# Low parts of the up-projection's weights made by adding DMAs, 1/rms on VectorE, a third tile for the weight sums, and P4's low products last

## The chip, the cores and the metric

The kernel runs on one core of a Trainium2 chip. The metric is device time in microseconds (us) of one execution, shown as the median of the runs with the lowest and the highest.

The core's engines work in parallel, each through its own queue in order: PE (TensorE: matmuls from on-chip memory into accumulators), DVE (VectorE: elementwise), ACT (ScalarE: one-input elementwise), POOL (GpSimd: elementwise, and it can issue DMAs), SP (SyncE: here it only issues DMAs). Engines wait for one another through semaphores. 16 DMA engines move data.

## The reference

One layer of a hybrid decoder on 1024 tokens with 1024 channels, in float32:

```python
xn = rmsnorm(x, norm_mix_w); proj = xn @ w_in
merged = sigmoid(g_da) * (y_da @ w_br_da) + sigmoid(g_sw) * (y_sw @ w_br_sw)   # two attentions
x = x + merged @ w_mix_out
xn = rmsnorm(x, norm_ffn_w)
u = xn @ w_up                                   # 1024 -> 2 * 2816 channels
c = conv_b + sum(upad[:, j:j + S] * conv_w[j] for j in range(3))   # causal, per channel
gate, val = split(c, 2)
x = x + (silu(gate) * val) @ w_down
out = rmsnorm(x, norm_final_w)
```

The change lies in the stage that computes `u` and the convolution with its gate.

## The kernel before, in words

**Three passes.** A float32 operand is split into a high part `h` (rounded to the matmul's format by a copy on ScalarE, a CAST in the profile) and a low part `l` = value - `h` (a subtraction on VectorE). A product of two operands is `wh*xh + wh*xl + wl*xh`: three matmuls for every 128 rows of the inner dimension.

**Seven products for eight.** The up-projection's 5632 output channels are worked off as 22 pairs of blocks of 128 channels: pair j holds block j (gate, called g) and block j + 22 (value, called v). The inner dimension is cut in two halves of four chunks, and the tokens in two halves of 512 as well. Instead of eight products per pair there are seven, P1 to P7, each of 12 matmuls (four chunks by three passes) into one 128x512 accumulator. Their weight operands are A11, A12 (the two halves of g), A22 (the second half of v) and four sums S1 to S4, made by four operations of POOL of 128x512 each (`sum_pair`): `sa` holds S1 and S2, `sb` holds S3 and S4. `recombine` adds the seven results up into two tiles `us` of 128x1024 on VectorE.

In the order of the loop a pair's products are P1 (A11), P2 (A12), P5 (S1), P6 (S2), P7 (S3), P3 (S4), P4 (A22). In `product`, `low_last=True` puts the four matmuls with the weights' low part behind the eight others; before, only P1 has that.

**High and low parts of a pair's weights** are made in `split_pair`: four splits a pair, of g (128x1024, tiles wh and wl), `sa` and `sb` (128x1024 each, tiles sh and sl) and the second half of v (128x512, tiles wh and wl of the pool `w22`). Buffers set the order: wh and wl of g have two, sh and sl three between `sa` and `sb`, A22's wh and wl one; g is loaded into "raw" (three buffers), v into "rv" (two), and the sums lie in "sf" (two tiles, one for `sa`, one for `sb`). SP issues both loads and stores the finished rows of h to `hd` in DRAM. `ahead` keeps two pairs of weights in preparation: while pair j is multiplied, pair j + 1 and a part of j + 2 are prepared.

**After the products.** `glu_halves` multiplies both `us` tiles by 1/rms (`rstd`; 128x1024 on POOL, line 1083; for the first pair on VectorE), clears two border columns (a memset on POOL, line 1082), and runs the convolution: an activation on ScalarE (line 1089) and two scaled additions on VectorE (line 1091) per tile and half, then silu and the product of both.

The instructions are laid out by a tile framework, which sets the order within each engine from the order in the program, its priorities and the buffers, and writes the semaphore waits.

Of the kernel before, what the change touches and what calls it, by code (L numbers as in the profile page):

```python
# [10 lines left out]
F32 = mybir.dt.float32  # L11
F32R = mybir.dt.float32r
AF = mybir.ActivationFunctionType
ALU = mybir.AluOpType
# [3 lines left out]
P = 128  # L18
# [6 lines left out]
NF = DFF // P  # L25
# [19 lines left out]
class Trunk:  # L45
    def __init__(self, tc, ins, out):
        self.tc, self.nc = tc, tc.nc
        (self.xT, self.w_in, self.w_br, self.w_mix, self.w_up, self.w_dn,
         self.vecs_d, self.bias_d) = ins
        self.out = out  # L50
        self.uid = 0
        self.stores = []
        self.uw = self.w22 = self.behind = None
        self.pin, self.after = False, None
        self.hs, self.defer, self.late = {}, [], []

    def name(self, s):
# [12 lines left out]
    def ahead(self, n):  # L70
        while len(self.wq) < n and self.wsrc and (self.wsrc[0][1] != "pair" or self.uw):
            src, nk, *eng = self.wsrc.pop(0)
            if nk == "sums":

                self.sums = self.split_pair(*self.sum_pair(src, True, "sl"), 1, 3)
            elif nk == "rest":
                self.sums["A22"] = self.load_w(src[1][:, 4:8], 4)
                self.wq.append(self.sums)
            elif nk == "second":
                self.wq.append(self.second_pair(src, *eng))  # L80
            elif nk == "idle":
                self.wq.append(self.load_w(src, 8, None, (self.uw, "sh", "sl")))
            elif nk == "pair":
                first, skip = eng or (False, 0)
                self.wq.append(self.split_pair(*self.sum_pair(src, first), skip))
            else:
                self.wq.append(self.load_w(src, nk, *eng))
        if self.deep and self.wsrc and len(self.wsrc[0]) == 2 and not isinstance(self.wsrc[0][1], str):

            src, nk = self.wsrc[0]  # L90
            self.wsrc[0] = src, nk, None, None, self.load_raw(src, nk)

    def sum_pair(self, src, first=False, idle=None):


        nc = self.nc
        g = self.tl(self.wp, [P, 2, 4, P], "raw", bufs=RAW)
        nc.sync.dma_start(g.rearrange("p a k c -> p (a k) c"), src[0])
        v = self.tl(self.wp, [P, 2, 4, P], "raw", bufs=RAW) if first and not idle else self.tl(self.uw, [P, 2, 4, P], idle or "rv", bufs=2)
        nc.sync.dma_start(v.rearrange("p a k c -> p (a k) c"), src[1])  # L100
        sa, sb = (self.tl(self.sfp[0], [P, 2, 4, P], self.sfp[1]) for _ in range(2))
        tt = nc.gpsimd.tensor_tensor
        i = tt(sa[:, 0], v[:, 0], v[:, 1], ALU.add)  # L103
        if self.behind is not None:
            self.tc.add_manual_dep(i.ins, self.behind.ins.name, mybir.DependencyInfo(mybir.DependencyClass.Sync, mybir.DependencyReason.DATA), reason="operands first")
            self.behind = None
        tt(sa[:, 1], sa[:, 0], g[:, 0], ALU.subtract)
        tt(sb[:, 0], g[:, 0], v[:, 0], ALU.subtract)  # L108
        tt(sb[:, 1], g[:, 1], sa[:, 1], ALU.subtract)
        return g, v, sa, sb  # L110

    def split_pair(self, g, v, sa, sb, skip=0, end=4):

        nc = self.nc
        ops = {}
        for pool, h, l, src, names in ((self.wp, "wh", "wl", g, ("A11", "A12")), (self.uw, "sh", "sl", sa, ("S1", "S2")),
                                       (self.uw, "sh", "sl", sb, ("S3", "S4")), (self.w22 or self.wp, "wh", "wl", v[:, 1:2], ("A22",)))[skip:end]:
            n = len(names)
            hi = self.tl(pool, [P, n, 4, P], h, F32R)
            lo = self.tl(pool, [P, n, 4, P], l, F32R)  # L120
            with ExitStack() as queue:
                if self.pin and ops:
                    for i in done:
                        queue.enter_context(self.tc.issue_after(i.ins))
                if self.after is not None and names[0] == "A11":
                    queue.enter_context(self.tc.issue_after(self.after.ins))
                i = nc.scalar.copy(hi, src)  # L127
                j = nc.vector.tensor_tensor(lo, src, hi.bitcast(F32), ALU.subtract)  # L128
            if not ops:
                done = i, j  # L130
            if names[0] in ("A11", "A22"):
                ops["made", names[0]] = i, j
            for i, name in enumerate(names):
                ops[name] = hi[:, i], lo[:, i]
        self.pin, self.after = False, None
        return ops
# [788 lines left out]
    def hidden(self, pair):  # L925
        nc, tc = self.nc, self.tc
        with ExitStack() as ctx:
# [11 lines left out]
            for j in range(NF):  # L939
                w, ps = ready.pop(j) if j else (w0, {})  # L940
                if j == 0:
# [4 lines left out]
                    for k in range(4):  # L946
                        hi, lo = self.split(*(xc2.tile([P, T], F32R, name=f"T42_{k}{p}") for p in "hl"), self.t42[k])
# [14 lines left out]
                if j == NF - 1:  # L962

                    with tc.high_priority(50):
# [4 lines left out]
                        lo = self.lo  # L969
                for name, a, b in (prods[i] for i in ((0, 1, 2, 5, 3, 6, 4) if j == NF - 1 else (0, 1, 2, 5, 3, 4, 6) if j else range(7))):  # L970
                    if name not in ps:
                        ps[name] = self.tl(*((self.psC, [P, H2], "c") if j == 0 and name == "P4" else (psF, [P, H2], "t")))
                        self.product(ps[name], w[a], b, low_last=name == "P1")
                us = [self.tl(tp, [P, T + 2], "us", bufs=3) for _ in range(2)]
                if j == NF - 1:
                    self.defer.pop(0)(lo)
# [9 lines left out]
                if j < NF - 1:  # L986

                    self.after = c21
                    w, ps = ready[j + 1] = self.next_w(), {}
# [87 lines left out]
    def glu_halves(self, j, us):  # L1077

        nc = self.nc
        col = lambda m, k: self.vecs[:, C_CW + 3 * m + k:C_CW + 3 * m + k + 1]  # L1080
        for w, u in enumerate(us):
            nc.gpsimd.memset(u[:, 0:2], 0.0)
            (nc.vector if j == 0 else nc.gpsimd).tensor_tensor(u[:, 2:], u[:, 2:], self.rstd, ALU.mult)  # L1083
        out = self.tl(self.cpl, [P, T], "c")
        for o in (0, H2):
            cs = [self.tl(self.psC, [P, H2], "c") for _ in range(2)]
            for w, (u, c) in enumerate(zip(us, cs)):
                m = j + w * NF
                nc.scalar.activation(c, u[:, o + 2:o + 2 + H2], AF.Identity, bias=self.vecs[:, C_CB + m:C_CB + m + 1], scale=col(m, 2))  # L1089
                for k in (1, 0):  # L1090
                    nc.vector.scalar_tensor_tensor(c, u[:, o + k:o + k + H2], col(m, k), c, ALU.mult, ALU.add)  # L1091
            g = out[:, o:o + H2]
            nc.scalar.activation(g, cs[0], AF.Silu)  # L1093
            nc.vector.tensor_tensor(g, g, cs[1], ALU.mult)
        nc.sync.dma_start(self.hd[j], out)
# [351 lines left out]
```

## Time and profile before

| what | value |
|---|---|
| median of 3 runs (lowest to highest) | 1343.09 us (1341.19 to 1344.43) |
| profiled execution: its time / its span | 1342.84 us / 1340.6 us |
| up-projection on TensorE, from its first matmul to the down projection's | about 684 to 1106 us of the span |
| mean granted TensorE clock | 0.997 of full speed |

A row of the profile's groups reads: line, engine, operation, output<-input tiles, shapes, count | busy us in all, mean ns of one | idle time of the engine just before these instructions and what ended it. A row in order of time gives start and duration in us. In the waits, "A <- B" says that A was idle until B had finished. PEld is the load of weights, which runs beside the matmuls.

### The profile page before, as it was taken

The page shows a single profiled execution, that of the slowest core. Times are in us where ns is not written, and L with a number is a line of the kernel's source. Part 1 is how long each engine was busy: PE and PEld are TensorE (multiplying, and loading weights), DVE is VectorE, ACT ScalarE, POOL GpSimd, SP SyncE. Part 2 cuts the span into 40 slices and gives each one's busy share as a digit, 9 for nine tenths or more (in the row PEclk, how much of TensorE's full clock was granted, in tenths as well). Part 3 has the DMA queues.
Part 4 walks back from the last instruction along what each step waited for, and adds up shares of the span by engine and source line. Part 5 has one row for each costly group of instructions (what it writes and reads, how often), then busy time and mean ns, then how long its engine had stood idle before and what let it go on. Part 6 is the DMA issues. An engine that isn't in the chain of part 4 may idle for free.

```text
span 1340.6 us, 17301 instructions
## 1 busy us (share of the span) xinstructions
PE 1319.9 (98%) x6264; PEld 1097.0 (82%) x6264; DVE 1069.3 (80%) x1605; ACT 621.2 (46%) x1019; POOL 497.0 (37%) x365
## 2 busy tenths in 40 slices
PE   8999999999999999999999999999999999999997
PEld 6888888888888777878888888888888888888787
DVE  8847775289889876465678999999999997978985
ACT  9432232276667765333444443444443444323454
POOL 0336553001102124651446555655565510215422
PEclk9999999999999999999999999999999999999998
DMA  7423443876553235334432222222222229671333
GB/s 258 145 107 143 156 158 141 246 182 186 144 135 124 97 119 203 141 110 157 126 110 95 78 95 79 94 68 90 90 85 80 85 82 337 214 263 63 112 124 126
DMA packets 63045, 182.64 MB, mean 136 GB/s; under 512 B 6896, under 2 KB 15216, under 8 KB 62960
## 3 DMA queue, kind: packets, MB, share of 16 engines
q1 hardware_dynamic: 51504, 164.13, 37.5%
q10 hardware_dynamic: 11456, 17.41, 3.6%
q8 instruction: 49, 0.80, 0.3%
q14 instruction: 36, 0.29, 0.1%
HBM read 130.66 MB, written 50.86 MB: 135 GB/s over the span
## 4 chain that ended last, share of the span: by engine, by line
PE 87%; POOL 4%; DVE 4%; DMA 3%; ACT 1%; issue 1%; POOLq 0%; SPq 0%; ACTq 0%; DVEq 0%
PE t L920 13%; PE t L921 13%; PE t L922 13%; PE g L209 3%; PE t L914 3%; PE g L210 3%; PE g L211 3%; PE sc L636 3%; PE y L1159 2%; PE d L1159 2%; DMA gr<-gd 2%; PE sc L211 2%; PE sc L209 2%; PE sc L210 2%; PE d L920 2%; PE d L921 2%
## 5 line engine op out<-in xcount | busy, mean ns | idle before, releaser
L1089 ACT ACTIVATE c<-us,vecs 128x512 f32<-128x512 f32 x80 | 61.3, 780 | 133.2 <-POOL us L1083 129.2
L1091 DVE SCALAR_TENSOR_TENSOR c<-us,vecs,c 128x512 f32<-128x512 f32 x160 | 110.4, 747 | 8.6 <-ACT c L1089 8.5
L1083 POOL TENSOR_TENSOR us<-us,rstd 128x1024 f32<-128x1024 f32 x38 | 99.7, 2643 | 4.5 <-DVE us L469 2.4
L128 DVE TENSOR_TENSOR sl<-sf,sh 128x1024 fp32r<-128x1024 f32 x62 | 87.6, 1415 | 11.5 <-ACT sh L127 11.5
L127 ACT CAST sh<-sf 128x1024 fp32r<-128x1024 f32 x62 | 63.3, 1048 | 60.2 <-PE t L921 43.7
L176 DVE TENSOR_TENSOR wl<-raw,wh 128x1024 fp32r<-128x1024 f32 (+2 forms) x46 | 55.7, 1210 | 31.8 <-ACT wh L174 20.2
L128 DVE TENSOR_TENSOR wl<-raw,wh 128x1024 fp32r<-128x1024 f32 (+1 forms) x35 | 76.3, 2180 | 3.7 <-ACT wh L127 3.6
L103 POOL TENSOR_TENSOR sf<-rv 128x512 f32<-128x512 f32 x30 | 41.3, 1378 | 100.9 <-DVE sl L128 57.8
L174 ACT CAST wh<-raw 128x1024 fp32r<-128x1024 f32 (+2 forms) x46 | 46.1, 1001 | 61.8 <-PE sc L210 30.5
L209 PE MATMUL g<-xh,wh 128*128 128x512 f32 x176 | 70.6, 401 | 0.1
L211 PE MATMUL g<-xh,wl 128*128 128x512 f32 x176 | 70.3, 400 | 0.0
L210 PE MATMUL g<-xl,wh 128*128 128x512 f32 x176 | 70.3, 399 | 0.0
L108 POOL TENSOR_TENSOR sf<-raw,rv 128x512 f32<-128x512 f32 x30 | 40.7, 1358 | 65.3 <-DVE sl L128 65.3
L619 POOL MEMSET aT<- 128x128 f32 x32 | 6.2, 206 | 151.6 <-PE t L665 101.3
L640 DVE CUSTOM_DVE_ANT_0 L<-sc,bias 128x128 f32<-128x128 f32 (+7 forms) x64 | 47.7, 751 | 17.0 <-PE sc L636 13.7
L641 ACT ACTIVATE L<-L,sm 128x128 f32<-128x128 f32 (+7 forms) x64 | 49.6, 778 | 20.0 <-DVE sm L640 17.3
L794 POOL TENSOR_TENSOR gr<-gr,rstd 128x1024 f32<-128x1024 f32 x16 | 40.6, 2540 | 42.5 <-DMA gr<-gd 42.3
L1093 ACT ACTIVATE c<-c 128x512 f32<-128x512 f32 x40 | 24.0, 599 | 60.7 <-DVE c L1091 60.7
L128 DVE TENSOR_TENSOR wl<-rv,wh 128x512 fp32r<-128x512 f32 x30 | 49.3, 1642 | 3.5 <-ACT wh L127 3.5
L636 PE MATMUL sc<-u,u 128*128 128x512 f32 (+2 forms) x192 | 49.8, 358 | 0.0
L211 PE MATMUL sc<-mh,wl 128*128 128x512 f32 x126 | 49.1, 390 | 0.5 <-DVE wl L176 0.5
L209 PE MATMUL sc<-mh,wh 128*128 128x512 f32 x126 | 49.0, 389 | 0.0
(527 smaller groups left out, 4400.3 us busy)
## 6 DMA issues: line engine op xcount, KB each, us to landing
u<-qd SPq DMA_DIRECT2D x72, 256.0 KB, 6.6
raw<-in_w_in SPq DMA_DIRECT2D x25, 512.0 KB, 4.2
raw<-in_w_up SPq DMA_DIRECT2D x23, 512.0 KB, 3.5
hr<-hd SPq DMA_DIRECT2D x46, 256.0 KB, 4.9
hd<-c SPq DMA_DIRECT2D x22, 512.0 KB, 2.6
rv<-in_w_up SPq DMA_DIRECT2D x21, 512.0 KB, 3.5
raw<-in_w_down SPq DMA_DIRECT2D x19, 512.0 KB, 4.2
gr<-gd SPq DMA_DIRECT2D x16, 512.0 KB, 3.7
```

The costliest lines, as they stand in the source:

```text
L127: i = nc.scalar.copy(hi, src)
L128: j = nc.vector.tensor_tensor(lo, src, hi.bitcast(F32), ALU.subtract)
L209: nc.tensor.matmul(ps, wh[:, kc + o, :], ah, start=first and n == 0, stop=False)
L210: nc.tensor.matmul(ps, wh[:, kc + o, :], al, start=False, stop=False)
L211: nc.tensor.matmul(ps, wl[:, kc + o, :], ah, start=False, stop=last and n == len(kcs) - 1)
L636: nc.tensor.matmul(sc[:, lo + n0:lo + n1], qs, k[c][part][:, n0:n1], start=part == 0, stop=part == 1)
L920: nc.tensor.matmul(ps, ah[:, k, :], bh, start=first and n == 0, stop=False, skip_group_check=skip)
L921: nc.tensor.matmul(ps, ah[:, k, :], bl, start=False, stop=False, skip_group_check=skip)
L922: i = nc.tensor.matmul(ps, al[:, k, :], bh, start=False, stop=last and n == len(ks) - 1, skip_group_check=skip)
L1083: (nc.vector if j == 0 else nc.gpsimd).tensor_tensor(u[:, 2:], u[:, 2:], self.rstd, ALU.mult)
L1089: nc.scalar.activation(c, u[:, o + 2:o + 2 + H2], AF.Identity, bias=self.vecs[:, C_CB + m:C_CB + m + 1], scale=col(m, 2))
L1091: nc.vector.scalar_tensor_tensor(c, u[:, o + k:o + k + H2], col(m, k), c, ALU.mult, ALU.add)
```

## The change

From the third pair of the up-projection on (j = 2 to 21), a low part is no longer a subtraction on VectorE: ScalarE writes -h into the low tile, and then a DMA issued from POOL's queue adds the value to it in place (`accum_op=ALU.add`). For these pairs `sb` lies in a tile "t42" of its own (one buffer), so that `sa` has both "sf" buffers to itself. The multiplication by 1/rms and the memset move from POOL to VectorE in all pairs of `glu_halves`. P4's four matmuls with the low part go last.

```diff
@@ ahead
             if nk == "sums":
+                self.by_dma = False
...
             elif nk == "pair":
                 first, skip = eng or (False, 0)
+                self.npairs += 1
+                self.by_dma = len(self.pairs) + 1 < self.npairs < len(self.pairs) + NF
@@ sum_pair
-        sa, sb = (self.tl(self.sfp[0], [P, 2, 4, P], self.sfp[1]) for _ in range(2))
+        sa, sb = (self.tl(self.sfp[0], [P, 2, 4, P], x, **k) for x, k in ((self.sfp[1], {}), ("t42", {"bufs": 1}) if self.by_dma else (self.sfp[1], {})))
@@ split_pair
                 i = nc.scalar.copy(hi, src)
-                j = nc.vector.tensor_tensor(lo, src, hi.bitcast(F32), ALU.subtract)
+                if self.by_dma:
+                    j = nc.scalar.mul(lo, hi.bitcast(F32), -1.0)
+                    nc.gpsimd.dma_start(lo, src, accum_op=ALU.add)
+                else:
+                    j = nc.vector.tensor_tensor(lo, src, hi.bitcast(F32), ALU.subtract)
@@ hidden
-                        self.product(ps[name], w[a], b, low_last=name == "P1")
+                        self.product(ps[name], w[a], b, low_last=name in ("P1", "P4"))
@@ glu_halves
-            nc.gpsimd.memset(u[:, 0:2], 0.0)
-            (nc.vector if j == 0 else nc.gpsimd).tensor_tensor(u[:, 2:], u[:, 2:], self.rstd, ALU.mult)
+            nc.vector.memset(u[:, 0:2], 0.0)
+            nc.vector.tensor_tensor(u[:, 2:], u[:, 2:], self.rstd, ALU.mult)
```

How POOL's queue stands in a regular pair, before (the first four sums and what lies between; us are the tiles that get 1/rms, rv and raw the loaded v and g):

```order
L103 TENSOR_TENSOR sf_7126<-rv_7124 128x512
L107 TENSOR_TENSOR sf_7126<-sf_7126,raw_7122 128x512
L1082 MEMSET us_7111 128x2
L108 TENSOR_TENSOR sf_7127<-raw_7122,rv_7124 128x512
L109 TENSOR_TENSOR sf_7127<-raw_7122,sf_7126 128x512
L1082 MEMSET us_7265 128x2
L1083 TENSOR_TENSOR us_7110<-us_7110,rstd 128x1024
L1083 TENSOR_TENSOR us_7111<-us_7111,rstd 128x1024
```

and now (line numbers are the changed kernel's; L134 is the adding DMA, and a tile named t_ with two numbers is "t42"):

```order
L107 TENSOR_TENSOR sf_7301<-rv_7299 128x512
L111 TENSOR_TENSOR sf_7301<-sf_7301,raw_7297 128x512
L134 DMA wl_7308<-raw_7297 128x1024
L134 DMA sl_7159<-t_1206_7143 128x1024
L112 TENSOR_TENSOR t_1234_7302<-raw_7297,rv_7299 128x512
L113 TENSOR_TENSOR t_1234_7302<-raw_7297,sf_7301 128x512
L134 DMA sl_7313<-sf_7301 128x1024
L134 DMA wl_7164<-rv_7140 128x512
```

The multiplications are gone, and two DMAs stand behind each two sums: the pair's own A11, A12 with the S3, S4 of the pair before, then the pair's own S1, S2 with the A22 of the pair before.

VectorE's queue in a regular pair, before, between two steps of `recombine` (L468, L469, L470 are its last ones; L128 the subtractions; L1091 the convolution):

```order
L468 TENSOR_TENSOR s_1285_7577<-t_7510,s_1285_7577 128x512
L469 TENSOR_TENSOR us_7575<-t_7549,s_1285_7577 128x512
L128 TENSOR_TENSOR sl_7602<-sf_7591,sh_7601 128x1024
L470 TENSOR_TENSOR us_7576<-u_1286_7578,t_7562 128x512
L128 TENSOR_TENSOR wl_7455<-rv_7434,wh_7454 128x512
L128 TENSOR_TENSOR wl_7598<-raw_7587,wh_7597 128x1024
L1091 SCALAR_TENSOR_TENSOR c_7618<-us_7575,vecs,c_7618 128x512
```

and now (L476, L477, L478 are the same steps of `recombine`, L1090 and L1091 the memset and 1/rms, L1099 the convolution):

```order
L476 TENSOR_TENSOR s_1257_7446<-t_7379,s_1257_7446 128x512
L1090 MEMSET us_7603 128x2
L477 TENSOR_TENSOR us_7444<-t_7418,s_1257_7446 128x512
L1091 TENSOR_TENSOR us_7444<-us_7444,rstd 128x1024
L478 TENSOR_TENSOR us_7445<-u_1258_7447,t_7431 128x512
L1091 TENSOR_TENSOR us_7445<-us_7445,rstd 128x1024
L1099 SCALAR_TENSOR_TENSOR c_7491<-us_7444,vecs,c_7491 128x512 x2
```

The subtractions are gone, and each `us` tile is multiplied right after its last step of `recombine`.

More of the change, by code (lines that the diff above doesn't have):

```diff
@@ L54, in __init__ @@
         self.pin, self.after = False, None
+        self.by_dma, self.npairs = False, 0
         self.hs, self.defer, self.late = {}, [], []
```

## The prediction, made before the changed kernel was run

> **What bounds the kernel now.** I read the page first, then the waits of TensorE, then the busy time by stretch, then the chain that ended last. The page:
>
> ```profile
> PE 1319.9 (98%) x6264; PEld 1097.0 (82%) x6264; DVE 1069.3 (80%) x1605; ACT 621.2 (46%) x1019; POOL 497.0 (37%) x365
> ```
>
> TensorE is busy for 1319.9 of 1340.6 us. Its own waits leave little to win; these two are the longest (waiting line, releaser, us in total, times, longest):
>
> ```profile
> PE t L340 <- ACT wh L174: 6.6, 1, 6.6
> PE y L920 <- DVE x L1285: 2.9, 1, 2.9
> ```
>
> The first is the start of the program, the second is in the down projection; neither is in the up-projection. Busy time by stretch (columns: stretch, length, PE, PEld, DVE, ACT, POOL, granted clock, DMA share, GB/s), the up-projection's steady part and all that follows:
>
> ```profile
> 700.00:1100.00 400.00, 399.91 (x1768) 331.06 (x1768) 381.02 (x446) 174.88 (x237) 218.31 (x168) 1.00 0.25 84
> 1100.00:1340.00 240.00, 230.79 (x1081) 192.60 (x1079) 195.49 (x256) 96.75 (x147) 65.68 (x41) 0.99 0.51 176
> ```
>
> In the stretch that the change edits, TensorE idles 0.09 us of 400. VectorE is nearly full too (381 of 400), but nobody on the path waits for it. The chain shows the beat, the first and the last product P1 of a regular pair:
>
> ```profile
> 724.81 1.81 PE t L914 x8
> 726.62 0.91 PE t L916 x4
> ...
> 1086.57 1.81 PE t L914 x8
> ```
>
> From 724.81 to 1086.57 are 19 pairs: 19.04 us a pair, seven products of 12 matmuls, each product 1.81 + 0.91 = 2.72 us. **Below 19.04 us a pair nothing can go**, since the change takes no matmul away. So the question is whether the new way of making low parts still keeps a beat of 19.04 us.
>
> **The change, part by part.** Group rows of a regular part of the stage (740 to 1090 us; busy us and mean ns of one stand behind the bar):
>
> ```profile
> L1083 POOL TENSOR_TENSOR us<-us,rstd 128x1024 f32<-128x1024 f32 x36 | 95.7, 2679 | 4.5 <-DVE us L469 2.4
> L128 DVE TENSOR_TENSOR wl<-raw,wh 128x1024 fp32r<-128x1024 f32 x18 | 53.7, 2985 | 0.0
> L128 DVE TENSOR_TENSOR sl<-sf,sh 128x1024 fp32r<-128x1024 f32 x37 | 46.8, 1264 | 0.0
> L127 ACT CAST sh<-sf 128x1024 fp32r<-128x1024 f32 x37 | 37.1, 1045 | 0.5 <-PE t L921 0.4
> L128 DVE TENSOR_TENSOR wl<-rv,wh 128x512 fp32r<-128x512 f32 x18 | 32.9, 1826 | 0.0
> L127 ACT CAST wh<-rv 128x512 fp32r<-128x512 f32 x19 | 11.8, 622 | 10.2 <-PE t L921 10.2
> ```
>
> *VectorE* loses, per pair, two subtractions at 1.26, one at 2.99 and one at 1.83 us: 7.34 us. It gains two multiplications by 1/rms of 128x1024, each between 1.26 us (the same shape, undisturbed) and 2.99 us (the same shape beside a running POOL operation): 2.5 to 6.0 us. From 381.02/400 x 19.04 = 18.1 us a pair it goes to 13.3 to 16.8. That buys nothing, as nobody waited. *ScalarE* gains three negations at about 1.05 and one at 0.62 us, like its casts: 8.3 + 3.8 = 12.1 us a pair, under 19.04, so it is hidden. *POOL* loses two multiplications of 2.68 us and gains four DMA issues. *P4's low products last*: the same 12 matmuls, no time by itself; A22's low part is needed at the ninth instead of the third matmul, 6 x 2.72/12 = 1.36 us later.
>
> The cost that matters is **a new ring of waits through POOL's queue**, read from the order above and the buffers. Per pair POOL now does: issue the add for S1, S2's low part and, right behind it, the one for A22's; two sums of the next pair; issue A11, A12's add and, right behind it, the one for S3, S4's; two more sums. The pair's v tile (two buffers of "rv") is read by A22's add, so the v after the next can be loaded only when that add has landed; the first sums wait for this load; the last sums write the only t42 tile, which the add of S3, S4's has just read, so they wait for that landing too. And both awaited adds stand second in their queue, behind another add. On SP, behind the v load that now waits for a DMA, stand the store of an earlier pair's h and the next g load, both needed a pair later; on ScalarE, behind a negation that waits for its buffer, stand the activations of the gated part, with 7 us a pair to spare. The fixed members, from POOL's and SP's instructions in order of time:
>
> ```profile
> 897.04 1.29 POOL L108 TENSOR_TENSOR sf<-raw,rv 128x512 f32<-128x512 f32 x1 [3.04 <-DVE sl L128]
> 898.29 1.30 POOL L109 TENSOR_TENSOR sf<-raw,sf 128x512 f32<-128x512 f32 x1
> 899.53 0.10 POOL L1082 MEMSET us<- 128x2 f32 x1
> ...
> 907.00 1.29 POOL L103 TENSOR_TENSOR sf<-rv 128x512 f32<-128x512 f32 x1 [1.92 <-DMA rv<-in_w_up]
> 908.37 1.30 POOL L107 TENSOR_TENSOR sf<-sf,raw 128x512 f32<-128x512 f32 x1
> ```
>
> ```profile
> 903.25 0.33 SPq L100 DMA_DIRECT2D rv<-in_w_up  x1
> ```
>
> The v load takes 907.00 - 903.25 = 3.75 us to its first reader, the first two sums 2.67 us (907.00 to 909.67), the last two 2.55 us (897.04 to 899.59): 8.97 us. (The memsets that leave POOL are 0.10 us each.)
>
> An adding DMA is in no row. The nearest are plain transfers of the same 512 KB (us from issue to landing) and a small operation of POOL:
>
> ```profile
> raw<-in_w_up SPq DMA_DIRECT2D x23, 512.0 KB, 3.5
> hd<-c SPq DMA_DIRECT2D x22, 512.0 KB, 2.6
> ```
>
> ```profile
> 704.74 1.14 POOL rs L229
> ```
>
> A pair moves three plain 512 KB transfers (two loads, one store of h), and the DMA share is 0.25: 0.25 x 19.04 / 3 = 1.59 us on all 16 engines each. So of the store's 2.6 us, 0.33 is issue, 1.59 moving, 0.68 the rest; of the load's 3.5 the rest is 1.58. For an add, moving (m) lies between 1.59 us (the second operand is read for nothing) and 3.18 us (two operands are read, one after the other). I take 3.18: it reads the target as well as the source, and a plain transfer reads once. Issue and rest together lie between 0.33 + 0.68 = 1.01 us (the store, which also starts in on-chip memory) and 1.14 + 1.58 = 2.72 us; I take 1.01, the row that it is nearest to.
>
> A22's add (256 KB) lands behind S1, S2's: 1.01 + 1.5m after the first's issue. S3, S4's lands behind A11, A12's: 1.01 + 2m. The ring is 8.97 + 2.02 + 3.5m. At m = 1.59 it is 16.6 us and fits; at **m = 3.18 it is 22.1 us, 3.1 us over the beat**; at 2.72 and 3.18 it is 8.97 + 5.44 + 11.13 = 25.5 us. It fits up to m = 2.30, 1.45 times a plain transfer.
>
> The Trainium skill, page "DMA: Bandwidth & Descriptors", section "Anatomy of one DMA — SWDGE (gpsimd) path", gives a DMA issued by GpSimd as 2.0 us plus its bytes over 436 GB/s; no run here shows it. An estimate by that page with every byte counted twice makes the ring 8.97 + 5.6 + 6.8 = 21.4 us, and the time some 1377 us; counted once, 17.2 us and no loss. The Trainium skill, page "Collectives: The Full Stack", section "The bandwidth ceiling: the fold count and why AG ≠ RS ≠ AR", says that an add in the DMA's path is slow for its two source reads and not for adding, a measured ratio of 1.93; that speaks against this change, and no run here shows it either.
>
> What slack is there? A22's add can go out once P4 of the pair before has ended and ScalarE has negated (0.62 us); with 5.8 us to land it is down 6.4 us into the pair. From there S3, S4's low part takes 3.75 + 2.67 + 7.4 = 13.8 us, and P7 of the next pair reads it at 19.04 + 4 x 2.72 + 0.45 = 30.4 us. 10.2 us may be lost before TensorE stands. The 20 changed pairs make 19 turns of the ring: 19 x 3.08 - 10.2 = 48 us. The profiled execution took 1342.84 us (its span 1340.6), 0.25 us from the median of the runs, 1343.09: **1342.8 + 48 = 1391 us**. At the upper price: 19 x 6.5 = 123, less some 8, gives 1458.
>
> **The rivals.** A time within 0.2% (2.7 us) of before counts as no change; a measurement of this kernel can hardly tell less.
>
> *The ring fits* (not slower). If the two reads overlap, so that m stays under 2.30 us with issue and rest at 1.01, POOL, VectorE and ScalarE all stay below 19.04 us, and TensorE keeps its beat: 1343 us. For it: DMA is busy a quarter of the time only, and the adds are issued well before their low parts are read. Against it: the two awaited adds both stand second in line. Chance 0.24.
>
> *Faster*. VectorE's relief could carry into the down projection and end the wait of 2.9 us for L1285: 1339.9 us, just beyond 0.2%. Against it: that wait lies some 150 us behind the stage, and VectorE is not full there (195 of 240 us). Chance 0.03.
>
> *POOL's issue is the price*. If VectorE's two-operand work holds up POOL's issue as POOL's work holds up VectorE's (2.99 for 1.26 us), each of the two multiplications a pair adds 1.26 us: the ring at its upper price becomes 28 us, 19 x 9.0 - 8 = 163 us, about 1506 us. Against it: POOL's own sums keep 1.30 us throughout. The Trainium skill, page "SBUF — State Buffer", section "SBUF: two separate sides", has this as a rule: GpSimd cannot write descriptors while VectorE holds the port that they share; the row of 2.99 us shows the sharing, but not for a DMA issue. Chance of anything above 1458: 0.15.
>
> **How the numbers follow.** The long ring has 0.58, from 1346 to 1458, likeliest 1391. The ring that fits has 0.24, faster 0.03, above 1458 0.15. The range from 1341 (the lowest run of before) to 1458 takes in the first two and leaves out under 2 in 10. Faster 0.03, same 0.24, slower 0.58 + 0.15 = 0.73.
>
> **What would show it.** Right: P1 of successive pairs stands about 22 us apart instead of 19.04 (the early ones still 19.04); TensorE's waits name DMAs into sl or wl, at P7 or P4; POOL's first sum waits for the v load and its later sum for a DMA; VectorE idles. Wrong: a beat of 19.04 us throughout (the add moves in under 2.30 us), a landing of the adds under 3 us, or a wait of TensorE for ScalarE or for VectorE, which this sum leaves at nothing.

## The result, and the profile after

The changed kernel took **1462.64 us** (median of 5 runs, 1459.17 to 1464.86); the kernel before, on the same chip, 1343.4 us (1341.19 to 1344.47). The ratio is **1.0887, 95% interval 1.0872 to 1.0903**: 119 us slower. The forecast was slower too, but by 48 us, and its range ended at 1458.

The page of the changed kernel, first its engines, then its DMA queues, then its chain by engine and by line:

```profile
PE 1362.4 (93%) x6264; PEld 1117.6 (77%) x6264; DVE 987.7 (68%) x1603; ACT 693.1 (48%) x1099; POOL 461.6 (32%) x367
...
q0 software_dynamic: 11520, 36.71, 13.0%
...
PE 57%; DMA 26%; POOL 10%; DVE 3%; issue 2%; ACT 1%; POOLq 0%; SPq 0%; ACTq 0%; DVEq 0%
DMA wl<-rv 9%; DMA sl<-t 8%; DMA rv<-in_w_up 5%; PE t L928 5%; PE t L929 5%; PE t L930 5%; PE g L217 3%; PE g L218 3%; PE g L219 3%; PE sc L644 2%; PE d L1167 2%; PE y L1167 2%; PE sc L219 2%; PE sc L217 2%; PE sc L218 2%
```

No engine is full any more: TensorE is busy for 93% of the span and VectorE fell to 68%. On the chain two adding DMAs and the v load are 22% of the span. q0 is the adds' queue. TensorE's waits:

```profile
PE t L924 <- DMA wl<-rv: 57.7, 18, 3.7
PE t L930 <- DMA sl<-t: 8.8, 8, 1.7
...
PE d L1167 <- DVE us L478: 4.4, 1, 4.4
```

TensorE waits for A22's low part (wl<-rv) at P4, in 18 of the pairs, and for that of S3, S4 (sl<-t) in eight. The beat shows in TensorE's matmuls by form, the first matmul of P1 (columns behind the count: shortest, median and longest in ns; start of the first and of the last):

```profile
L922 PE MATMUL t<-B_0h,wh x18: 387/628/632, 742.5 to 1164.3; 128*128 128x512 f32 x18
```

Seventeen beats in 421.8 us are 24.81 us each, for 19.04 before. In that stretch the chain holds no matmul at all. One turn of it, the chain of waits in order of time:

```profile
907.95 0.54 POOL sl L134
908.49 7.37 DMA wl<-rv
...
915.92 4.13 DMA rv<-in_w_up
...
920.20 1.26 POOL sf L107
...
921.54 1.28 POOL sf L111
922.83 0.53 POOL wl L134
923.36 6.37 DMA sl<-t
...
929.80 0.33 POOL t L112
...
931.06 1.29 POOL t L113
932.35 0.54 POOL sl L134
932.89 7.33 DMA wl<-rv
```

This is the predicted ring, member for member: A22's add behind that of S1, S2; the v load; two sums; the add of S3, S4 behind that of A11, A12; two sums. From 907.95 to 932.35 it takes 24.4 us. The landings of its DMAs (KB, median us from issue to landing), where h's store (hd<-c) took 2.6 us before:

```profile
hd<-c SPq DMA_DIRECT2D x22, 512.0 KB, 5.3
rv<-in_w_up SPq DMA_DIRECT2D x21, 512.0 KB, 4.3
sl<-sf POOLq DMA_DIRECT2D x20, 512.0 KB, 6.7
wl<-raw POOLq DMA_DIRECT2D x20, 512.0 KB, 4.5
sl<-t POOLq DMA_DIRECT2D x20, 512.0 KB, 6.4
wl<-rv POOLq DMA_DIRECT2D x20, 256.0 KB, 7.4
```

The smallest add, A22's 256 KB, takes longest to land.

### The profile page after: what moved, and what is told of

The parts are those of the page before. It is cut to its first block, busy times and chain, and to the rows that moved or that the text cites. A ratio compares the mean times of both kernels' runs of the same rounds, so it can differ in the third digit from the quotient of the medians.

```text
span 1457.3 us, 17505 instructions
## 1 busy us (share of the span) xinstructions
PE 1362.4 (93%) x6264; PEld 1117.6 (77%) x6264; DVE 987.7 (68%) x1603; ACT 693.1 (48%) x1099; POOL 461.6 (32%) x367
## 4 chain that ended last, share of the span: by engine, by line
PE 57%; DMA 26%; POOL 10%; DVE 3%; issue 2%; ACT 1%; POOLq 0%; SPq 0%; ACTq 0%; DVEq 0%
DMA wl<-rv 9%; DMA sl<-t 8%; DMA rv<-in_w_up 5%; PE t L928 5%; PE t L929 5%; PE t L930 5%; PE g L217 3%; PE g L218 3%; PE g L219 3%; PE sc L644 2%; PE d L1167 2%; PE y L1167 2%; PE sc L219 2%; PE sc L217 2%; PE sc L218 2%
## 5 line engine op out<-in xcount | busy, mean ns | idle before, releaser
L1099 DVE SCALAR_TENSOR_TENSOR c<-us,vecs,c 128x512 f32<-128x512 f32 x160 | 118.7, 753 | 139.2 <-ACT c L1097 134.5
L131 ACT CAST sh<-sf 128x1024 fp32r<-128x1024 f32 x42 | 44.1, 1052 | 280.2 <-POOL sf L111 234.5
L924 PE MATMUL t<-T_0h,wl 128*128 128x512 f32 x21 | 12.2, 582 | 57.7 <-DMA wl<-rv 57.7
L112 POOL TENSOR_TENSOR t<-raw,rv 128x512 f32<-128x512 f32 x20 | 25.8, 1292 | 98.7 <-DMA sl<-t 98.7
L1091 DVE TENSOR_TENSOR us<-us,rstd 128x1024 f32<-128x1024 f32 x40 | 50.5, 1266 | 6.3 <-ACT rstd L1013 5.1
L924 PEld LDWEIGHTS t<-T_0h,wl 128*128 128x128 f32 x21 | 4.6, 220 | 65.4 <-DMA wl<-rv 65.3
L218 PE MATMUL sc<-ml,wh 128*128 128x512 f32 x126 | 49.0, 389 | 0.0
L478 DVE TENSOR_TENSOR us<-u,t 128x512 f32<-128x512 f32 x30 | 20.5, 684 | 39.8 <-PE t L924 38.1
```

Source lines behind the costliest of these rows:

```text
L218: nc.tensor.matmul(ps, wh[:, kc + o, :], al, start=False, stop=False)
L1091: nc.vector.tensor_tensor(u[:, 2:], u[:, 2:], self.rstd, ALU.mult)
```

## The experiments

Each kernel is the changed one with the edit shown, and ran beside the kernel before on the same chip. Beat is the usual distance of two P1 in the later pairs.

| kernel | edit | us (before) | ratio, 95% interval | beat |
|---|---|---|---|---|
| e1_no_adds | no adds | 1347.55 (1342.81) | 1.0033, 1.0024 to 1.0043 | 19.04 |
| e4_plain_dma | plain copies for adds | 1386.86 (1342.81) | 1.0321, 1.0306 to 1.0337 | 21.2 |
| e2_a22_vector | A22 on VectorE | 1376.12 (1342.81) | 1.0237, 1.0218 to 1.0256 | 20.9 |
| e5_g_behind_v | g load behind v load | 1415.38 (1342.45) | 1.0548, 1.0532 to 1.0563 | 22.1 |
| e2b | e2 and e5 together | 1343.54 (1342.45) | 1.0009, 0.9999 to 1.002 | 19.04 |
| e3_s34_vector | S3, S4 on VectorE | 1358.64 (1343.57) | 1.0113, 1.0095 to 1.0131 | 19.0 to 19.9 |
| e6_awaited_first | awaited add first | 1382.87 (1342.81) | 1.0299, 1.028 to 1.0318 | 21.0 |
| e6b | e6 and e5 together | 1372.63 (1342.45) | 1.0233, 1.0215 to 1.025 | 20.2 |
| e7_p4_only | P4's order alone | 1358.93 (1342.45) | 1.0127, 1.0111 to 1.0142 | 19.7 |
| e11_p4_inline | P4 as before | 1439.18 (1343.57) | 1.0722, 1.0704 to 1.0739 | 23.9 |
| e12_p4_inline_order | e11, POOL's order kept | 1472.4 (1343.43) | 1.0959, 1.094 to 1.0979 | 25.6 |
| e9_until20 | adds end two pairs earlier | 1442.79 (1343.57) | 1.0742, 1.0724 to 1.076 | 25.0 |
| e10_two_tiles | no third tile | 1453.65 (1343.57) | 1.0825, 1.0803 to 1.0846 | 25.0 |

### Is it the adds at all? (e1_no_adds)

```diff
-                if self.by_dma:
+                if False:
```

> All low parts are made by VectorE's subtraction again; 1/rms on VectorE, the t42 tile and P4's low products last stay. Theory (the whole loss is the ring of waits that goes through the adding DMAs): no ring, beat 19.04 us, time of before, 1343 us within 4. Rival (VectorE is overfilled by 1/rms): 18.1 + 2.5 us a pair is 20.6, 1.6 us over the beat, some 19 x 1.6 = 30 us more, about 1373 us.

Measured 1347.55 us: of the 119 us some 115 come from the adds. A rest of 0.33% is left for 1/rms on VectorE, the third tile and P4's order together, 1.8 us of it at the second pair and 2.2 us at the end of the stage, where TensorE now waits for VectorE's steps:

```profile
PE d L1167 <- DVE us L477: 2.2, 1, 2.2
PE c L243 <- DVE us L474: 1.8, 1, 1.8
```

### What an add costs beside a copy (e4_plain_dma)

The low parts are copied and not added to, so the low products are wrong in value; everything else is as in the changed kernel.

```diff
-                    nc.gpsimd.dma_start(lo, src, accum_op=ALU.add)
+                    nc.gpsimd.dma_start(lo, src)
```

> As the changed kernel, but the DMAs from POOL's queue copy the value over the low tile instead of adding to it (the low parts are then not subtracted: the result is not the reference's). Theory (the ring is long because an add moves longer than a copy, 2.71 us of all 16 engines against 1.66 for a 512 KB transfer): ring 24.8 - 3.5 x 1.05 = 21.1 us, 17 x 2.1 + 16 = 52 us over before, about 1395 us. Rival (what is dear is a DMA issued from POOL's queue at all, its issue and its landing): no change, 1455 to 1465 us.

The queue of the adds and their landings, with copies in their place:

```profile
q0 software_dynamic: 11520, 36.71, 7.3%
...
wl<-raw POOLq DMA_DIRECT2D x20, 512.0 KB, 2.9
...
wl<-rv POOLq DMA_DIRECT2D x20, 256.0 KB, 5.8
```

The 20 pairs move 3.5 units of 512 KB each, 70 in all. An add takes 13.0% x 1457.3 / 70 = 2.71 us on all engines, a copy 7.3% x 1386 / 70 = 1.45 us: **1.87 times**. (The Trainium skill, page "Collectives: The Full Stack", section "The bandwidth ceiling: the fold count and why AG ≠ RS ≠ AR", gives a measured 1.93 between a collective without and one with an add in the DMA's path; the trace's 1.87, from 1.85 to 1.89 within the rounding of its shares, lies 3% below that.) Even plain copies leave the ring at 21.2 us, over 19.04: the adding is a part of the price, the ring is the rest.

### Which member of the ring? (e2, e5, e2b, e3)

First A22's add was taken away:

```diff
-                if self.by_dma:
+                if self.by_dma and names[0] != "A22":
```

> As the changed kernel, but A22's low part is subtracted on VectorE; 60 of the 80 adding DMAs stay. Theory (ring): v's buffer comes free without a DMA, so the first sums no longer wait for an add and a load in a row; what is left of the ring is 2.65 (sums) + 0.55 (issue) + 6.4 (S3, S4's add) + 2.55 (sums) + 0.55 = 12.7 us, under 19.04: 1343 to 1348 us, no wait of TensorE for a DMA. Rival (the adds cost by their number, through traffic, issue or the clock): three quarters of the 119 us stay, about 1432 us.

A miss: 1376.12 us. SP's and POOL's queues in order of time show why:

```profile
900.97 0.33 SPq L102 DMA_DIRECT2D raw<-in_w_up  x1
901.40 0.37 SPq L104 DMA_DIRECT2D rv<-in_w_up  x1
```

```profile
900.89 0.87 POOL L134 DMA_DIRECT2D sl<-sf  x1
909.76 1.28 POOL L107 TENSOR_TENSOR sf<-rv 128x512 f32<-128x512 f32 x1 [8.00 <-DMA rv<-in_w_up]
```

The v load no longer waits for A22's add, but it stands in SP's queue behind a g load that waits for POOL's last sums; then g load, v load and the add of S1, S2 go out within 0.5 us, and the v load lands in 8 us. A second ring of waits lay right behind the first: 8.8 us from 900.97 to the first sum, then 2.65 for two sums, 6.95 for the next couple of adds and 2.55 for two sums, as in the changed kernel: in sum 20.9.

Then the g load alone was moved behind the v load, in the changed kernel:

```diff
+        with self.tc.issue_after(self.vl[-2].ins) if self.by_dma and len(self.vl) > 1 else nullcontext():
             nc.sync.dma_start(g.rearrange("p a k c -> p (a k) c"), src[0])
```

> As the changed kernel, but SP issues each g load behind the v load that stood behind it, so that it no longer starts at the same moment as the adds of S1, S2's and A22's. Same adds, same loads. Theory (A22's add lands 2.1 us late because a 512 KB load runs beside the couple): beat 24.8 - 2.1 = 22.7 us, 17 x 3.7 + 16 = 79 us over before, about 1422 us. Rival (the two adds take that long alone): no change, 1455 to 1465 us.

```profile
sl<-sf POOLq DMA_DIRECT2D x20, 512.0 KB, 4.4
...
wl<-rv POOLq DMA_DIRECT2D x20, 256.0 KB, 5.2
```

Both adds of that couple land 2.2 to 2.3 us earlier than in the changed kernel (6.7 and 7.4), and the beat falls to 22.1. So some 2.2 of the 7.4 us of A22's add came from the g load, issued in the same moment. With both edits:

> A22's low part on VectorE as in the second experiment, and each g load behind the v load on SP. Theory (in the second experiment a ring was left because the v load stood on SP behind a g load that waits for POOL's last sums: 8.8 us from those sums to the first sums, then 2.65, then the couple's 6.95, then 2.55, is 20.9 of the 21.0 measured): with the v load ahead that member goes and 12.7 us are left, so the beat is 19.04 and the time that of the kernel without adds, 1347 to 1352 us. Rival (the 60 adds cost by themselves): stays at 1372 to 1378 us.

```profile
700.00:1100.00 400.00, 400.00 (x1769) 330.93 (x1768) 319.53 (x463) 232.41 (x297) 174.53 (x149) 1.00 0.66 163
```

1343.54 us: no idle time of TensorE in 400 us, at a DMA share of 0.66, the highest but two of all these kernels (0.61 in the changed kernel, in the same stretch), with 60 of the 80 adds still there. **It is the ring, not the traffic and not the adds as such**; traffic counts only where it lengthens a member of the ring. (The columns are those of the busy time by stretch.) It is also the best that this change can do, since TensorE is then as full as before; no version here beats the kernel before.

The other awaited add, on VectorE instead:

```diff
-                if self.by_dma:
+                if self.by_dma and names[0] != "S3":
```

> The changed kernel, but the low part of S3 and S4 is subtracted on VectorE; the adds for A11,A12, for S1,S2 and for A22 stay (50 of 70 units of 512 KB). Theory (the ring's members each cost what the changed kernel's trace shows): the last sums no longer wait for the landing of S3,S4's add, only for VectorE's subtraction, which is done early; of the ring's 24.8 us there stay A22's add 7.9 - 7.4 + 0.5, v load 4.3, first sums 2.65, one issue 0.55, last sums 2.55, one issue 0.55: about 18.5 us. It fits into 19.04, so 1347 to 1365 us, and a beat of 19.04 to 19.5 us. Rival (it is the adds' traffic, not the ring): a quarter to a third of the traffic goes and 2/3 to 3/4 of the loss stays, about 1425 to 1432 us.

1358.64 us, as the ring has it. The rest of 15 us is a beat up to 19.9 and two last pairs of 22.8 and 22.2 us. The members left are A22's 0.54 + 7.5, the v load's 4.1, two sums (2.6 us in the turn shown, 3.4 in most), an issue and two sums that take longer here, 1.69 and 2.27 us for 1.29 each. The first stands right behind an issue (it takes 1.6 us there also in turns with VectorE idle), the second beside VectorE's multiplication by 1/rms:

```profile
899.50 1.69 POOL L112 TENSOR_TENSOR t<-raw,rv 128x512 f32<-128x512 f32 x1
901.15 2.27 POOL L113 TENSOR_TENSOR t<-raw,sf 128x512 f32<-128x512 f32 x1
```

### Awaited adds first (e6, e6b)

The adds of S3, S4 and of A22 each go out ahead of the one that they stood behind.

```diff
+                    front = self.adds.get({"A11": "S3", "S1": "A22"}.get(names[0]))
+                    with self.tc.issue_after(front.ins) if front is not None else nullcontext():
+                        self.adds[names[0]] = nc.gpsimd.dma_start(lo, src, accum_op=ALU.add)
-                    nc.gpsimd.dma_start(lo, src, accum_op=ALU.add)
```

> As the changed kernel, but in each of the two couples of adds the one that POOL or the v load waits for is issued first: S3, S4's ahead of A11, A12's, and A22's ahead of S1, S2's. Same adds, same bytes. Theory (ring; the second of a couple lands about 2.6 us after the first): 24.8 - 2 x 2.6 = 19.6 us, nearly the beat: 1350 to 1372 us. Rival (traffic: the adds and the loads together fill the DMA engines, or TensorE's clock): same bytes, same time, above 1440 us.

```profile
sl<-t POOLq DMA_DIRECT2D x20, 512.0 KB, 4.5
wl<-rv POOLq DMA_DIRECT2D x20, 256.0 KB, 5.7
```

1382.87 us, slower than the 1350 to 1372 expected: standing second cost 1.9 us for S3, S4 (6.4 to 4.5) and 1.7 for A22 (7.4 to 5.7), not more, as A22's add still shares the engines with the g load. With that load out of the way too:

> All 80 adds, the awaited one of each couple first, and each g load behind the v load on SP. Theory: the beat of 21.0 us with the awaited adds first loses the collision of A22's add with the g load (it landed in 5.7 us; 3.2 without), 18.5 us, so it fits into 19.04: 1347 (no adds) plus up to 10 at the end of the stage, 1347 to 1357 us. Rival (what is left over the beat is traffic or TensorE's clock): above 1375 us.

```profile
rv<-in_w_up SPq DMA_DIRECT2D x21, 512.0 KB, 5.6
...
wl<-rv POOLq DMA_DIRECT2D x20, 256.0 KB, 3.2
```

```profile
921.80 2.05 POOL L108 TENSOR_TENSOR sf<-rv 128x512 f32<-128x512 f32 x1 [7.30 <-DMA rv<-in_w_up]
923.93 2.16 POOL L112 TENSOR_TENSOR sf<-sf,raw 128x512 f32<-128x512 f32 x1
```

A miss as well, 1372.63 us. A22's add lands in 3.2 us, but of the 2.5 us gained only 0.8 reach the beat (21.0 to 20.2): the v load now runs beside the add of S1, S2 and the g load and takes 5.6 us for 4.4, and the first two sums take 4.0 us in the mean of twelve turns (840 to 1080 us), for 3.3 in e6 and 2.65 in the changed kernel, since they fall beside VectorE's multiplications by 1/rms. A member that ends sooner moves the next into other traffic.

### P4's order (e7, e11, e12)

In the kernel before, with P4's low products last and nothing else of the change (no adds, no third tile, 1/rms on POOL):

```diff
-                        self.product(ps[name], w[a], b, low_last=name == "P1")
+                        self.product(ps[name], w[a], b, low_last=name in ("P1", "P4"))
```

> The kernel before with P4's low products last as its one change. Theory (the 4.7 us that stayed without any adds come from 1/rms on VectorE, at the first and the last pair, where TensorE waited 1.8 and 2.2 us for VectorE): 1343 us, within 0.2% of before. Rival (P4's order costs): 1347 us.

```profile
PE t L928 <- DVE s L471: 6.7, 16, 1.0
```

A miss: 1358.93 us. TensorE waits for a step of `recombine` in 16 pairs. VectorE is not fuller there (260 of 300 us from 780 to 1080, for 291 before), but the step comes later. It is not P4's order alone: e1_no_adds has it too and keeps 19.04 us. The two differ in the place of 1/rms and in the third tile; which of the two does it was not tried.

And the changed kernel with that line alone as before:

> The changed kernel, but P4's products with the low part stand where they stood before, in the order of the chunks. Theory (the ring sets the beat, TensorE only follows): nothing or a little from the first stall, 1460 to 1467 us, beat 24.8 us. Rival (TensorE's own order counts, since A22's low part is needed 1.36 us earlier in each of 17 pairs): 1463 + 23 = 1486 us.

A miss in the other direction: 1439.18 us, 23 us faster than the changed kernel. POOL's queue in order of time (the idle time ahead and its releaser in brackets):

```profile
915.91 0.87 POOL L134 DMA_DIRECT2D wl<-raw  x1
916.52 1.67 POOL L111 TENSOR_TENSOR sf<-sf,raw 128x512 f32<-128x512 f32 x1
918.15 0.87 POOL L134 DMA_DIRECT2D sl<-t  x1
923.02 1.29 POOL L112 TENSOR_TENSOR t<-raw,rv 128x512 f32<-128x512 f32 x1 [4.00 <-DMA sl<-t]
```

The framework puts the add of A11, A12 between the two sums, 2.24 us ahead of that of S3, S4 and not 0.59. The second one then lands in 4.8 us for 6.4. The edit to P4 had moved an instruction on POOL. To tell this from TensorE's own order, the last kernel keeps e11's order on TensorE and puts that add back:

```diff
-        tt(sa[:, 1], sa[:, 0], g[:, 0], ALU.subtract)
+        self.sum2 = tt(sa[:, 1], sa[:, 0], g[:, 0], ALU.subtract)
...
+                    with self.tc.issue_after(self.sum2.ins) if names[0] == "A11" else nullcontext():
                         nc.gpsimd.dma_start(lo, src, accum_op=ALU.add)
```

> P4's products in the order of the chunks, as in the kernel e11_p4_inline (1439 us), but the add for A11 and A12 is held behind the pair's second sum, where it stands in the changed kernel; TensorE's queue is then that of e11, POOL's that of the changed kernel. Theory (the 23 us that e11 gained come from POOL's order: there the add of A11, A12 goes out 2.2 us ahead of the add of S3, S4 in place of 0.6, and the second lands in 4.8 us in place of 6.4): back to 24.8 us a pair and 1458 to 1467 us. Rival (TensorE's own order of P4 is what gained): 23.5 us a pair and 1436 to 1443 us.

1472.4 us: POOL's order is worth 33 us (1439 to 1472), so the theory holds in its main part. It is above the 1467 expected, and 10 us above the changed kernel, from which it differs in the regular pairs by P4's order on TensorE alone. In 16 of its 18 turns the second sum takes 2.15 us and not 1.28 (in the changed kernel in one of 18), each time beside VectorE's multiplication by 1/rms; in the two others VectorE is idle beside it. One such turn, on POOL and on VectorE:

```profile
954.09 2.15 POOL L111 TENSOR_TENSOR sf<-sf,raw 128x512 f32<-128x512 f32 x1
```

```profile
953.16 1.94 DVE L1091 TENSOR_TENSOR us<-us,rstd 128x1024 f32<-128x1024 f32 x1
```

These 0.87 us are the 0.8 us by which e12's beat is longer (25.6 for 24.8). So P4's low products last gain those 10 us by where a sum of POOL falls, while their effect on POOL's order costs 33. The place of that sum was not changed by itself.

### The end of the stage and the third tile (e9, e10)

```diff
-                self.by_dma = len(self.pairs) + 1 < self.npairs < len(self.pairs) + NF
+                self.by_dma = len(self.pairs) + 1 < self.npairs < len(self.pairs) + NF - 2
```

> The changed kernel, but its adds end two pairs earlier (18 changed pairs in place of 20). Theory (17 long turns at 5.8 us, and some 16 us at the end of the stage that come from the last pairs' adds having to land before the down projection): 15 turns stay, the last two pairs run at 19.04 us, and the end loses little: 1343 + 15 x 5.8 = 1430, to 1437 us. Rival (the end's loss comes from the order of the last pair, not from its adds): only the two turns go, 1463 - 12 = about 1450 us.

1442.79 us lies between the two: 16 long beats were left, not 15, and then 20.9, 19.04 and 21.9 us. Of the 16.4 us that the last two pairs lose in the changed kernel, 2.9 stay in the last.

```diff
-("t42", {"bufs": 1}) if self.by_dma else (self.sfp[1], {})
+(self.sfp[1], {})
```

> The changed kernel without its third tile: S3 and S4 lie in the two "sf" buffers again, beside S1 and S2. Theory (the sums wait for the same landings in the same order, whichever tile they lie in: the last sums for the add of S3,S4 of the pair before, the first for the v load that waits for A22's add, which goes out behind S1,S2's): no change, 1455 to 1470 us. Rival (the third tile is what closes the ring, or what loosens it): over 10 us either way, below 1453 or above 1473 us.

1453.65 us (2 runs), 1.4 us under the range of the theory, with a beat of 25.0 us as the theory has it: the third tile does nothing for the ring. Of the 5.2 us between the profiled executions (spans of 1457.3 and 1452.1 us) 4.7 stand in the last pair (21.9 for 26.6 us).

## Why the prediction was wrong

The mechanism held. TensorE's beat grows, its waits name DMAs into wl and sl at P4 and P7, POOL's first sum waits for the v load and its later one for a DMA, VectorE idles, and 1/rms costs VectorE 1.25 us a tile. The rival that the ring fits fell, and so did the one in which VectorE relieves the down projection (TensorE's wait there is 2.9 us as before). The time lies where the third rival put its chance, above 1458, but not by its mechanism: POOL's issue keeps its 0.53 to 0.55 us to the next piece in every turn of the chain, and 1/rms its 1.25 us. (The Trainium skill, page "SBUF — State Buffer", section "SBUF: two separate sides", says that GpSimd cannot write descriptors while VectorE works in a mode that takes the port that they share; whether VectorE's work here is of that kind no run shows, and beside it the issues of the changed kernel keep 0.58 to 0.61 us from one to the next.)

The loss in the profiled executions is 1457.3 - 1340.6 = 116.7 us of span: 17 x (24.81 - 19.04) = 98.1 in the regular pairs, 8.8 and 7.6 in the last two, 2.2 elsewhere. These are the 19 turns that the prediction counted, and all of them are long. Its sum gave 48.3 us. Of the 68.4 us that it lacks, 51.1 are the turn (19 x 2.69), 10.2 the slack, 4.9 what the last two pairs lose beyond two such turns (16.4 - 2 x 5.77), and 2.2 lie elsewhere. So three terms of the sum were mis-sized, the turn above all.

**The turn, 22.1 us predicted, 24.4 in the turn shown (24.81 in the mean).** The sums (2.67 and 2.55) measured 2.63 and 2.55. The moving of an add, taken as 3.18, is 2.71; its issue and rest, taken as 1.01, are 4.5 - 2.71 = 1.8, in the middle of the bounds and not at the row of the store. These two errors cancel: 8.97 + 2 x 1.8 + 3.5 x 2.71 = 22.1 again. What is missing is company. A22's couple takes 7.97 us (907.95 to 915.92) for 1.8 + 4.07, because SP issues the g load in the same moment,

```profile
907.97 0.33 SPq L102 DMA_DIRECT2D raw<-in_w_up  x1
```

and the v load takes 4.28 us to its first reader for 3.75. That is 2.6 us a turn, against 0.25 that the couple of S3, S4 takes less than 1.8 + 5.42; e5 took the first part away and got 2.7 back. The prediction priced each add with the engines to itself and its couple, although the very sums that release the add of S1, S2 also release that load.

**The slack, 10.2 us predicted, none.** It assumed that the first A22's add goes out 0.62 us behind P4 of the pair before, at 742.5 - 19.04 + 0.6 = 724.1. POOL's queue of the changed kernel at that place:

```profile
723.96 0.88 POOL L134 DMA_DIRECT2D sl<-t  x1 [4.10 <-ACT sl L133]
728.47 1.30 POOL L112 TENSOR_TENSOR t<-raw,rv 128x512 f32<-128x512 f32 x1 [3.64 <-DMA sl<-t]
...
731.57 1.15 POOL L134 DMA_DIRECT2D wl<-rv  x1
```

It went out at 731.57, since in POOL's queue it stands behind the add of S3, S4, which waits for ScalarE's negation, and behind two sums that wait for that add's landing. 7.5 us of the slack were gone before the first turn, the first turn took the rest, and TensorE stood already in the second of the changed pairs: the first distance of two P1 in them is 19.0 us, the second 25.5.

**The end of the stage, two turns like the others predicted, 16.4 us measured.** Two turns of the measured beat would lose 11.5. The next stage's first step on ScalarE needs a buffer that A22's add reads, and the activations and casts of the last pairs stand behind it:

```profile
1187.55 0.62 ACT L841 CAST rv<-sf 128x512 fp32r<-128x512 f32 x1 [12.29 <-DMA wl<-rv]
```

With the adds gone from the last two pairs (e9) all but 2.9 us are gone, the two turns and the rest together; that this buffer makes the rest is read from the row and was not tried by itself.

**P4's low products last, "no time by itself".** With this edit the framework puts two adds next to each other in POOL's queue, which costs 33 us, and the turn gets back 10 (e12); why the framework does so no run shows. In all the edit costs 23 us here (e11) and 16 in the kernel before (e7). The prediction's turn had the two adds next to each other, read from the order as given; the question which edit put them there was not asked.

At the upper price, 25.5 us a turn less some 8 of slack, the prediction's own sum gave 1458. The turn stayed under that price, so the end of the range was missed by the slack and the end of the stage; the likeliest value was missed mostly by the turn, which the g load and the v load's company made longer.

## What to carry to other kernels

An operation moved to a DMA leaves an engine's time and enters a queue of waits: follow the buffers round until they close into a ring, add its members up against the beat, and give each DMA the price that it has beside whatever the same event releases on other queues. Slack is counted from where the first instruction stands in its queue, not from when its operands are ready. An edit to one engine's order has to be looked up in every engine's order; here the one that touched only TensorE's lines moved POOL.

## What the runs showed of the hardware

- An adding DMA from on-chip to on-chip memory moves 512 KB in 2.71 us on all 16 engines where a copy takes 1.45, and as the first of its couple it lands in 4.5 us for 2.9 (changed, e4). (The Trainium skill, page "DMA: Bandwidth & Descriptors", section "Anatomy of one DMA — SWDGE (gpsimd) path", gives 2.0 us plus bytes over 436 GB/s, an estimate of 3.2 us for 512 KB and of 4.4 with every byte counted twice: near both rows.)
- The same 256 KB add lands in 3.2, 5.2, 5.7 or 7.4 us (e6b, e5, e6, changed): ahead of the other add of its couple, behind it, ahead of it but beside a 512 KB load, and behind it beside that load.
- A 128x512 sum on POOL takes 1.29 us, and 2.15 when it starts beside VectorE's multiplication by 1/rms; beside VectorE's additions of the convolution it keeps 1.29 (e12).
- After most of its longer waits TensorE is slow for some microseconds. A wait of 3.75 us and what follows, in order of time:

```profile
1015.49 0.79 PE L924 MATMUL t<-T_0h,wl 128*128 128x512 f32 x1 [3.75 <-DMA wl<-rv]
...
1020.35 0.63 PE L922 MATMUL t<-B_3l,wh 128*128 128x512 f32 x1
1020.78 0.44 PE L924 MATMUL t<-B_0h,wl 128*128 128x512 f32 x1
```

  A matmul every 0.43 us for some 5 us, and 0.23 us before and after; the granted clock is 0.50 from 1015.5 to 1020.5 us and 1.00 from 1021.2 on. From 740 to 1085 us the mean granted clock is 0.93. In e5, whose waits in that stretch last 2.0 us at most, it is 1.00, and three of the 18 waits here, of 2.2 to 2.5 us, leave it at 1.00 too. TensorE's busy time rose by 42.5 us for the same 6264 matmuls (1319.9 to 1362.4). Here that filled time in which TensorE would have waited anyway, since the ring set the beat.
- Where TensorE is the bound, a stall costs more than its own length: in e7 16 waits of 6.7 us in all stand beside beats longer by 0.66 us, 10.6 us in 16 pairs, at a granted clock of 1.00.
